# Gate projections of a two-branch mixer: spread over its units, with the results parked in DRAM

## The chip, the cores and the metric

One Trainium2 chip, one core. The metric is the device time of one execution in microseconds (us); the median of three timed runs counts. A separate execution is profiled, and all rows below come from it. Engines: PE (TensorE, matrix multiplication), DVE (VectorE), ACT (ScalarE), POOL (GpSimd), SP (the queue that issues DMAs).

## What is computed

Three blocks run one after the other on one sequence of 512 positions and 1024 channels. The change touches the third block's mixer only. It has two branches, a gated delta rule (GDN) and RWKV-7; each branch's output is multiplied by a gate that is a sigmoid of a projection of the block's input `h`, and the two are added:

```
p = h @ w_in[i]
qkv_a, z_a, b_a, a_a, p_b, gl_a, gl_b = split_cols(p, IN_SIZES)
y_a = gated_deltanet(qkv_a, z_a, b_a, a_a, conv_gdn[i], a_log[i], dt_bias[i], onorm_gdn[i])
y_b = rwkv7_time_mix(p_b, mu_rwkv[i], w0[i], w2[i], a0[i], a2[i], g2[i], k_k[i], k_a[i],
                     r_k[i], lnx_w[i], lnx_b[i])
y_a = y_a.astype(x.dtype) @ w_branch_gdn[i]
y_b = y_b.astype(x.dtype) @ w_branch_rwkv[i]
merged = jax.nn.sigmoid(gl_a) * y_a + jax.nn.sigmoid(gl_b) * y_b
x = x + gate1 * (merged @ w_out[i])
```

`gl_a` and `gl_b` have 1024 columns each, so there are 8 + 8 gate projections of 128 columns.

## The kernel before

Everything is feature-major: a tile is 128 channels by 512 positions. A projection (`proj_h`) loads one weight of 128 × 1024 (512 KB) on SP, splits it into a high half (cast on ACT, L310) and a low half (subtraction on DVE, L312), and runs 24 matmuls of 512 columns on PE into one of three PSUM banks named `pj` (L325 to L327). The buffers hold two raw weights, three high and three low halves.

The mixer works in eight units, four pairs of heads for each branch. A unit has three steps: `a` (projections, convolution or token shift, normalisation), `b` (scores, and `tri_inv`, which inverts eight 128 × 128 triangular matrices: a 16-step solve on DVE over the transposed diagonal blocks `iv_ld`, then small matmuls on PE, the first of them at L1820) and `d` (the recurrence over four chunks). The table `MIX3` writes down the order in which the steps are emitted: `ra0` is RWKV, step a, pair 0; `gd3` is GDN, step d, pair 3. `s0` to `s7` are the gate projections of the RWKV branch (weights 39 to 46), `t0` to `t7` those of the GDN branch (weights 31 to 38), `u0` to `u3` the merges of the RWKV branch's output. `PR3` gives each kind a number; emission is moved ahead by that number in the scheduler's priorities (`ahead`), and the scheduler then sets the order on each engine. On each engine instructions run in that order.

A gate is `sigmoid_of`: ACT takes Abs (L426, from PSUM), Exp (L429), Ln (L430), DVE the log-sigmoid (L434, from PSUM), ACT the last Exp (L1551). Before the change the results are written where they are used: `gr` (RWKV) in a state tile `s8z[2]`, in `lo`, `sg1`, `sg2` and one tile of the kind `f2`; `gg` (GDN) in two `f2` tiles, an `f4` tile and a state tile. All these are in use by the units for most of the mixer. The names in the trace are without the kernel's digits: `s`, `s_lo`, `s_sg` and `x_gate` are gate tiles, `x_yp` the split branch outputs, `ps_pj` a projection's bank. After the last unit the GDN branch is merged (8 merges of 12 matmuls), the sum is split into `hh` and `hl`, and `w_out` is applied.

Of the kernel before, what the change touches and what calls it, by code (L numbers as in the profile page):

```python
# [10 lines left out]
F32 = mybir.dt.float32  # L11
# [18 lines left out]
TAKE2 = 1  # L30
TAKE3 = 2
FILL2 = [4, 6, 8, 8]
PR3 = {"a": 0, "b": 400, "d": 500, "s": 300, "p": 150, "t": 300, "u": 0}
MIX3 = ("ra0 rb0 ra1 rd0 ga0 rb1 gb0 rd1 ra2 rb2 gd0 ga1 gb1 rd2 ra3 rb3 gd1 ga2 gb2 rd3 ga3 s0 s1 s2"
        " s3 gb3 s4 gd2 s5 s6 u0 t0 s7 u1 u2 u3 t1 t2 t3 t4 t5 t6 gd3 t7").split()

# [193 lines left out]
def dview(t, off, dims):  # L232

    return bass.AP(tensor=t.tensor, offset=t.offset + off, ap=[list(t.ap[0])] + [list(d) for d in dims])


class K:
# [1374 lines left out]
    def mix3(self):  # L1612
        nc, tc, I = self.nc, self.tc, self.I
        W = I["w_in_3"]
        stt = nc.vector.scalar_tensor_tensor
        with ExitStack() as st:
# [6 lines left out]
            with ExitStack() as sx:  # L1623
# [4 lines left out]
                f2 = lambda: self.p3.tile([P, S], F32, tag="f2", name="x3_gate", bufs=4)  # L1628
                s4 = lambda i: [self.s8z[i].rearrange("p (a b) c t -> p a (b c t)", a=4)[:, j, :] for j in range(4)]
# [10 lines left out]

                gr, gg, up = None, None, None
                for k in MIX3:
                    if k[0] == "s":
                        if gr is None:
                            gr = s4(2) + [self.lo, self.sg1, self.sg2, f2()]
                        m = int(k[1])
                        with self.ahead(PR3["s"]):
                            self.sigmoid_of(gr[m], self.proj_h(W[39 + m]))
                        continue
                    if k[0] == "t":  # L1650
                        if gg is None:
                            f4 = self.p3.tile([P, 2, S], F32, tag="f4", name="x3_gate2", bufs=2)
                            gg = [f2(), f2(), f4[:, 0, :], f4[:, 1, :]] + s4(self.niv % 2)
# [44 lines left out]
    def small3(self):  # L1698

        nc, I = self.nc, self.I  # L1700
        W = I["w_in_3"]
        p3, tmp = self.p3, self.tmp
        tt, stt, act, ts = nc.vector.tensor_tensor, nc.vector.scalar_tensor_tensor, nc.scalar.activation, nc.vector.tensor_scalar
# [20 lines left out]
        e = tmp("s3_e")  # L1724
# [14 lines left out]
        gr = self.gr = p3.tile([40, S], F32R, name="s3_gr")  # L1739
# [27 lines left out]
        h = slice(0, 64)  # L1767
# [10 lines left out]
        act(sg1, sg1, AF.Exp)  # L1778

        zt = lambda name, shape: p3.tile(shape, F32, name=name)  # L1780
        self.lc, self.xd = zt("iv_lc", [P, 32, 32]), zt("iv_xd", [P, 32, 32])
        self.Y = [zt("iv_Y0", [P, 8, P]), zt("iv_Y1", [P, 8, P])]
        self.x64 = zt("iv_x64", [P, 8, 64])
        self.Sb = [zt("ch_S0", [P, P]), zt("ch_S1", [P, P])]
# [6 lines left out]
    def tri_inv(self, LA):  # L1791


        nc, p3 = self.nc, self.p3
        tt, mm = nc.vector.tensor_tensor, nc.tensor.matmul
# [2 lines left out]
        self.niv += 1  # L1798
        q4 = [slice(32 * q, 32 * q + 32) for q in range(4)]
        for q in q4:  # L1800
            nc.scalar.mul(lc[q, 0:8, :], LA[q, :, 0, q], -1.0)
        iv = lambda name: p3.tile([P, 32, 32], F32, tag="iv", name=name, bufs=2)
        ld = iv("iv_ld")
        nc.vector.transpose(ld.rearrange("p t s -> p t s"), lc.rearrange("p h t -> p t h"))
        for i in range(1, 16):
            m = self.tmpd("iv_m", [P, 2, i, i])
            tt(m, dview(ld, 32 * i, [[528, 2], [0, i], [1, i]]), dview(xd, 0, [[528, 2], [1, i], [32, i]]), op=ALU.mult)  # L1807
# [376 lines left out]
```

## Time and profile before

| | |
|---|---|
| timed runs, us | 3452.67, 3456.22, 3472.29 (median 3456.22) |
| profiled execution, us | 3489.37 |
| its span, us | 3487.6 |
| mean granted TensorE clock over the span | 0.968 |
| PE, DVE, ACT busy, us | 3347.3, 2423.6, 1809.2 |
| the mixer's units, us from the start | about 2484 to 3010 |

The span is the time from the first to the last instruction. Busy time of PE is modelled at its ends, and a busy PE may still run at half of its clock, so the granted clock is read beside it (1.00 is 2.4 GHz, 0.50 is 1.2 GHz). Times in rows count from the start of the span.

### The profile page before, as it was taken

The numbers are of one execution on the slowest core, as the hardware profiler recorded it, in microseconds if no ns is written. First come the engines' busy times: TensorE is split into PE (matmuls) and PEld (weight loads), VectorE is DVE, ScalarE is ACT, GpSimd is POOL, SyncE is SP. The second block draws the span as 40 slices with busy tenths as digits, with TensorE's granted clock in tenths as the row PEclk, the third lists the DMA queues.
The fourth block names the chain that finished last, engine by engine and source line by source line (L and its number), as shares of the span: only waits on it lengthen the run. The fifth ranks groups of instructions, "written<-read, shape, count | busy, mean of one in ns | idle before, by whom it ended". The sixth has DMA issues, their size and how long they took to land.

```text
span 3487.6 us, 50543 instructions
## 1 busy us (share of the span) xinstructions
PE 3347.3 (96%) x20168; PEld 2672.4 (77%) x20168; DVE 2423.6 (69%) x3873; ACT 1809.2 (52%) x3020; POOL 123.6 (4%) x56
## 2 busy tenths in 40 slices
PE   7999999999799999999999999999899999999998
PEld 5888888888577777776787778878667667878887
DVE  6697767877789988677665465544767778565545
ACT  6566656566544555555455543334645556544434
POOL 0000000000132330000000000000000000000000
PEclk9999999999899999999999999999979989999999
DMA  6233333321121223334322245542201101323332
GB/s 224 91 96 100 97 95 96 107 85 56 44 72 61 68 72 97 121 106 130 100 73 67 85 135 184 171 151 97 96 23 50 40 31 38 109 90 95 95 96 85
DMA packets 109662, 325.08 MB, mean 93 GB/s; under 512 B 12721, under 2 KB 13361, under 8 KB 108786
## 3 DMA queue, kind: packets, MB, share of 16 engines
q1 hardware_dynamic: 109170, 321.06, 28.6%
q8 instruction: 158, 2.59, 0.3%
q0 software_dynamic: 256, 0.79, 0.1%
q14 instruction: 78, 0.64, 0.1%
HBM read 315.51 MB, written 6.29 MB: 92 GB/s over the span
## 4 chain that ended last, share of the span: by engine, by line
PE 76%; DVE 15%; ACT 4%; DMA 2%; issue 2%; SPq 0%; POOL 0%; DVEq 0%; ACTq 0%
PE ps_pj L326 19%; PE ps_pj L325 19%; PE ps_pj L327 19%; DMA ada_raw<-ada_w 2%; DVE w_lo L312 2%; DVE iv_m L1807 1%; PE ps_o L1443 1%; PE ps_mx L2098 1%; DVE ada_acc L493 1%; ACT w_hi L310 1%; PE ps_ad L496 1%; DVE iv_xd L1808 1%; PE ps_mx L326 1%; DVE cv_ul L318 1%; PE ps_mx L327 1%
## 5 line engine op out<-in xcount | busy, mean ns | idle before, releaser
L325 PE MATMUL ps_pj<-hh,w_hi 128*128 128x512 f32 x2344 | 940.0, 402 | 19.9 <-ACT hh L397 18.9
L326 PE MATMUL ps_pj<-hl,w_hi 128*128 128x512 f32 x2344 | 938.0, 400 | 0.0
L327 PE MATMUL ps_pj<-hh,w_lo 128*128 128x512 f32 x2344 | 934.8, 399 | 0.0
L310 ACT CAST w_hi<-w_raw 128x1024 fp32r<-128x1024 f32 (+1 forms) x435 | 454.6, 1045 | 761.5 <-PE ps_pj L326 661.4
L312 DVE TENSOR_TENSOR w_lo<-w_raw,w_hi 128x1024 fp32r<-128x1024 f32 (+1 forms) x387 | 469.9, 1215 | 312.9 <-ACT w_hi L310 305.9
L325 PEld LDWEIGHTS ps_pj<-hh,w_hi 128*128 128x128 f32 x2344 | 446.5, 191 | 130.1 <-ACT hh L397 24.5
L326 PEld LDWEIGHTS ps_pj<-hl,w_hi 128*128 128x128 f32 x2344 | 446.6, 191 | 101.3 <-issue 11.5
L327 PEld LDWEIGHTS ps_pj<-hh,w_lo 128*128 128x128 f32 x2344 | 446.0, 190 | 101.2 <-issue 10.9
L493 DVE SCALAR_TENSOR_TENSOR ada_acc<-ada_raw,sv_t_c,ada_acc 128x512 f32<-128x512 f32 x224 | 167.2, 746 | 55.0 <-DMA ada_raw<-ada_w 53.3
L967 DVE SCALAR_TENSOR_TENSOR xT<-ps_pj,ad,xT 128x512 f32<-128x512 f32 x128 | 95.4, 748 | 156.9 <-PE ps_pj L327 156.4
L312 POOL TENSOR_TENSOR w_lo<-w_raw,w_hi 128x1024 fp32r<-128x1024 f32 x48 | 121.1, 2523 | 1175.6 <-ACT w_hi L310 1175.6
L909 DVE SCALAR_TENSOR_TENSOR ps_mx<-cv_ut,vec,ps_mx 128x448 f32<-128x448 f32 (+3 forms) x192 | 128.1, 668 | 1.9 <-PE ps_mx L327 1.0
L909 DVE SCALAR_TENSOR_TENSOR ps_ad<-cv_ut,vec,ps_ad 128x480 f32<-128x480 f32 (+2 forms) x192 | 128.3, 668 | 1.6 <-ACT ps_ad L898 0.5
L325 PE MATMUL ps_pj<-w_hi,hh 128*128 128x256 f32 x416 | 120.3, 290 | 0.8 <-ACT hh L397 0.6
L327 PE MATMUL ps_pj<-w_hi,hl 128*128 128x256 f32 x416 | 118.7, 287 | 2.5 <-DVE hl L398 2.5
L326 PE MATMUL ps_pj<-w_lo,hh 128*128 128x256 f32 x416 | 121.0, 292 | 0.0
L326 PE MATMUL ps_pj<-m_yl,w_hi 128*128 128x512 f32 x256 | 100.4, 392 | 0.0
L325 PE MATMUL ps_pj<-m_yh,w_hi 128*128 128x512 f32 x256 | 100.3, 392 | 0.0
L327 PE MATMUL ps_pj<-m_yh,w_lo 128*128 128x512 f32 x256 | 100.3, 392 | 0.0
L327 PEld LDWEIGHTS ps_pj<-w_hi,hl 128*128 128x128 f32 x416 | 80.7, 195 | 3.9 <-DVE hl L398 3.2
L325 PEld LDWEIGHTS ps_pj<-w_hi,hh 128*128 128x128 f32 x416 | 80.8, 194 | 3.1 <-ACT hh L397 1.4
L326 PEld LDWEIGHTS ps_pj<-w_lo,hh 128*128 128x128 f32 x416 | 80.8, 194 | 1.9 <-issue 1.1
(793 smaller groups left out, 6486.9 us busy)
## 6 DMA issues: line engine op xcount, KB each, us to landing
ada_raw<-ada_w SPq DMA_DIRECT2D x288, 256.0 KB, 3.1
w_raw<-w_in SPq DMA_DIRECT2D x97, 512.0 KB, 3.7
w_raw<-hgrn_w_in SPq DMA_DIRECT2D x64, 512.0 KB, 3.7
w_raw<-w_mlp SPq DMA_DIRECT2D x64, 512.0 KB, 3.7
w_raw<-conv_w_in SPq DMA_DIRECT2D x48, 512.0 KB, 3.7
w_raw<-w_ffn_in SPq DMA_DIRECT2D x44, 512.0 KB, 3.5
w_raw<-hgrn_w_v SPq DMA_DIRECT2D x16, 512.0 KB, 3.6
w_raw<-hgrn_w_out SPq DMA_DIRECT2D x16, 512.0 KB, 3.6
```

Source lines behind the costliest of these rows:

```text
L310: nc.scalar.copy(hi, raw)
L312: (nc.gpsimd if self.on_pool else nc.vector).tensor_tensor(lo, raw, hi.bitcast(F32), op=ALU.subtract)
L318: self.nc.vector.tensor_tensor(lo, src, hi.bitcast(F32), op=ALU.subtract)
L325: mm(out, wh, xh, start=first, stop=False)
L326: mm(out, wh, xl, start=False, stop=False)
L327: mm(out, wl, xh, start=False, stop=last)
L493: nc.vector.scalar_tensor_tensor(acc, raw, cond[:, k:k + 1], acc, op0=ALU.mult, op1=ALU.add)
L496: nc.tensor.matmul(col[:, b:b + 1], acc[:, 128 * b:128 * b + 128], self.c("ones")[:, 0:1], start=True, stop=True)
L909: stt(o, x, tap(j), o, op0=ALU.mult, op1=ALU.add)
L967: self.nc.vector.scalar_tensor_tensor(self.xT[:, m, :], acc, gate[:, m:m + 1], self.xT[:, m, :], op0=ALU.mult, op1=ALU.add)
L1443: mm(out[64 * g:64 * g + 64, 128 * s:], vt[:, s, 128 * b + 64 * g:128 * b + 64 * g + 64], pts[g][:, c:c + S - 128 * s], start=b == 0 and s ...
L1807: tt(m, dview(ld, 32 * i, [[528, 2], [0, i], [1, i]]), dview(xd, 0, [[528, 2], [1, i], [32, i]]), op=ALU.mult)
```

## The change

`MIX3` gets a new order in which the gates stand between the units' steps from the beginning on, and `PR3` gives them −50, which lets them be taken later than what stands around them. As their final tiles are not free that early, 14 of the 16 gates are written to a tile `x_park` (one buffer, 2 KB a partition) and stored in DRAM (`g_spill`). At `S` the eight RWKV gates are loaded into their tiles, at `T` the first six GDN gates; `t6` and `t7` come behind `T` and go straight into theirs. The room for `x_park` comes from `iv_lc`, which shrinks from 32 × 32 to 8 × 32 a partition; the transpose into `iv_ld` reads its eight blocks four times instead of eight blocks and 24 blocks of zeros.

```diff
-PR3 = {"a": 0, "b": 400, "d": 500, "s": 300, "p": 150, "t": 300, "u": 0}
+PR3 = {"a": 0, "b": 400, "d": 500, "s": -50, "p": 150, "t": -50, "u": 0}
-        " s3 gb3 s4 gd2 s5 s6 u0 t0 s7 u1 u2 u3 t1 t2 t3 t4 t5 t6 gd3 t7").split()
+        " s7 ga3 S t1 gb3 t2 gd2 t3 u0 t4 u1 t5 u2 u3 T t6 gd3 t7").split()
...
+        self.parked = [self.dram.tile([P, S], F32, name="g_spill%d" % m) for m in range(16)]
...
-                    if k[0] == "s":
-                        if gr is None:
-                            gr = s4(2) + [self.lo, self.sg1, self.sg2, f2()]
+                    if k == "T":
+                        f4 = self.p3.tile([P, 2, S], F32, tag="f4", name="x3_gate2", bufs=2)
+                        gg = s4(self.niv % 2) + [f4[:, 0, :], f4[:, 1, :], f2(), f2()]
+                        for m in range(6):
+                            nc.sync.dma_start(gg[m], self.parked[8 + m])
+                        continue
+                    if gg is not None and k[0] == "t":
                         m = int(k[1])
                         with self.ahead(PR3["s"]):
-                            self.sigmoid_of(gr[m], self.proj_h(W[39 + m]))
+                            self.sigmoid_of(gg[m], self.proj_h(W[31 + m]))
                         continue
...
+                    if k[0] in "st":
+
                         m = int(k[1])
-                        with self.ahead(PR3["t"]):
-                            self.sigmoid_of(gg[m], self.proj_h(W[31 + m]))
+                        with self.ahead(PR3[k[0]]):
+                            e = self.p3.tile([P, S], F32, tag="park", name="x3_park", bufs=1)
+                            self.sigmoid_of(e, self.proj_h(W[(39 if k[0] == "s" else 31) + m]))
+                            nc.sync.dma_start(self.parked[m + (0 if k[0] == "s" else 8)], e)
+                        continue
+                    if k == "S":
+                        gr = s4(2) + [self.lo, self.sg1, self.sg2, f2()]
+                        for m in range(8):
+                            nc.sync.dma_start(gr[m], self.parked[m])
                         continue
...
-        self.lc, self.xd = zt("iv_lc", [P, 32, 32]), zt("iv_xd", [P, 32, 32])
+        self.lc, self.xd = zt("iv_lc", [P, 8, 32]), zt("iv_xd", [P, 32, 32])
...
-        nc.vector.transpose(ld.rearrange("p t s -> p t s"), lc.rearrange("p h t -> p t h"))
+        nc.vector.transpose(dview(ld, 0, [[32, 32], [8, 4], [1, 8]]), dview(lc, 0, [[1, 32], [0, 4], [32, 8]]))
```

Three places show how the program order moves. The first is DVE directly behind the last GDN output (`x_y<-ps_ad` of `gd3`); L434 is a gate's log-sigmoid, L312 a weight's low half, L318 a split of `y`. Before:

```order
L318 TENSOR_TENSOR x_yp<-x_y,x_yp 128x512
L312 TENSOR_TENSOR w_lo<-w_raw,w_hi 128x1024
L434 SCALAR_TENSOR_TENSOR x_gate_25686<-ps_pj,x_gate_25686 128x512
L312 TENSOR_TENSOR w_lo<-w_raw,w_hi 128x1024
L434 SCALAR_TENSOR_TENSOR s_0_21024<-ps_pj,s_0_21024 128x512
L312 TENSOR_TENSOR w_lo<-w_raw,w_hi 128x1024
L434 SCALAR_TENSOR_TENSOR s_0_21024<-ps_pj,s_0_21024 128x512
L312 TENSOR_TENSOR w_lo<-w_raw,w_hi 128x1024
L434 SCALAR_TENSOR_TENSOR s_0_21024<-ps_pj,s_0_21024 128x512
L312 TENSOR_TENSOR w_lo<-w_raw,w_hi 128x1024
L1571 TENSOR_TENSOR x_gate<-x_gate,ps_pj 128x512
L434 SCALAR_TENSOR_TENSOR s_0_21024<-ps_pj,s_0_21024 128x512
```

The same place of the change, from that output on (L2016 there):

```order
L2016 SCALAR_TENSOR_TENSOR x_y<-ps_ad,vec_20837,gd_gz 128x512
L312 TENSOR_TENSOR w_lo<-w_raw,w_hi 128x1024
L318 TENSOR_TENSOR x_yp<-x_y,x_yp 128x512
L434 SCALAR_TENSOR_TENSOR x_gate<-ps_pj,x_gate 128x512
L312 TENSOR_TENSOR w_lo<-w_raw,w_hi 128x1024
L434 SCALAR_TENSOR_TENSOR x_gate<-ps_pj,x_gate 128x512
L1572 TENSOR_TENSOR s_0_21040<-s_0_21040,ps_pj 128x512
```

Five gates stood behind the last unit's output, two stand there now. The second place is SP at the beginning of the mixer, from the last of the small loads on. Before:

```order
L274 DMA cst_b3s<-cst_b3s 128x392
L308 DMA w_raw<-w_in 128x1024 x33
L308 DMA w_raw<-w_br_r 128x1024
L308 DMA w_raw<-w_in 128x1024 x2
L308 DMA w_raw<-w_br_r 128x1024 x3
```

And of the change (L1661 is a store of a parked gate, L1666 a load at `S`; `g_spill_91` is `s0`):

```order
L274 DMA cst_b3s<-cst_b3s 128x392
L308 DMA w_raw<-w_in 128x1024 x7
L1661 DMA g_spill_91<-x_park 128x512
L308 DMA w_raw<-w_in 128x1024 x3
L1661 DMA g_spill_92<-x_park 128x512
L308 DMA w_raw<-w_in 128x1024 x5
L1661 DMA g_spill_93<-x_park 128x512
L308 DMA w_raw<-w_in 128x1024
L1661 DMA g_spill_94<-x_park 128x512
L308 DMA w_raw<-w_in 128x1024 x8
L1661 DMA g_spill_95<-x_park 128x512
L308 DMA w_raw<-w_in 128x1024 x2
```

Stores, which wait for ACT, now stand between the weight loads. The third place is ACT of the change near the end of the units, where three gates (`t1` to `t3`) follow closely; in brackets stands what an instruction waits for (DMAHW is a DMA's landing, for `x_park` that of the store before). Before, the gates there wait for no DMA.

```order
L1552 ACTIVATE x_park<-x_park 128x512 [waits DVE_49]
L310 CAST w_hi<-w_raw 128x1024 [waits DMAHW6_49]
L1811 ACTIVATE iv_lc<-s_1_21041 32x256 [waits DVE_49]
L1811 ACTIVATE iv_lc<-s_1_21041 32x256 x3
L310 CAST w_hi<-w_raw 128x1024 [waits DMAHW7_49,PE_49]
L426 ACTIVATE x_park<-ps_pj 128x512 [waits DMAHW2_49,PE_49,Activation_49]
L429 ACTIVATE x_park<-x_park 128x512 [waits Activation_49]
L430 ACTIVATE x_park<-x_park 128x512 [waits Activation_49]
L1552 ACTIVATE x_park<-x_park 128x512 [waits DVE_49]
L310 CAST w_hi<-w_raw 128x1024 [waits DMAHW3_49,PE_49]
L310 CAST w_hi<-w_raw 128x1024 [waits DMAHW4_49,PE_49]
L426 ACTIVATE x_park<-ps_pj 128x512 [waits DMAHW5_49,PE_49,Activation_49]
```

A gate's first operation on `x_park` waits for the store of the gate before it, and it stands in ACT's queue ahead of weight casts.

## Rows read from the trace of the kernel before

**Rows 1.** The page: span, busy time of engines, chain that ended last.

```profile
span 3487.6 us, 50543 instructions
...
PE 3347.3 (96%) x20168; PEld 2672.4 (77%) x20168; DVE 2423.6 (69%) x3873; ACT 1809.2 (52%) x3020; POOL 123.6 (4%) x56
...
PE 76%; DVE 15%; ACT 4%; DMA 2%; issue 2%; SPq 0%; POOL 0%; DVEq 0%; ACTq 0%
```

**Rows 2.** Windows of block 3's mixer: busy time (instructions), granted clock, DMA.

```profile
core 0: us, PE busy (x) PEld busy (x) DVE busy (x) ACT busy (x) POOL busy (x), PEclk, DMA share, GB/s
2484.00:3010.00 526.00, 493.26 (x4220) 365.99 (x4220) 393.11 (x781) 293.67 (x580) 1.62 (x3) 0.90 0.14 43
3010.00:3060.00 50.00, 48.53 (x213) 39.44 (x211) 29.34 (x38) 26.28 (x37) 0.00 (x0) 1.00 0.42 143
3060.00:3104.00 44.00, 44.00 (x195) 36.38 (x194) 21.27 (x28) 13.78 (x17) 0.00 (x0) 1.00 0.30 100
```

**Rows 3.** PE's waits, 2484 to 3010: releaser, us in total, times, longest.

```profile
PE ps_mx L1820 <- DVE iv_xc L1810: 9.4, 7, 3.7
PE ps_pa L1881 <- DVE rw_B L2064: 6.4, 2, 4.6
PE ps_ad L1978 <- DVE gd_y L1976: 3.8, 3, 1.7
```

**Rows 4.** Windows of 10 us in the units.

```profile
2550.00:2560.00 10.00, 6.14 (x215) 5.29 (x216) 9.77 (x15) 7.58 (x16) 0.00 (x0) 0.69 0.06 20
2560.00:2570.00 10.00, 10.00 (x85) 7.10 (x85) 2.77 (x5) 4.48 (x10) 0.00 (x0) 0.50 0.18 54
2570.00:2580.00 10.00, 10.00 (x42) 7.51 (x41) 2.99 (x5) 3.15 (x6) 0.00 (x0) 0.50 0.00 0
2580.00:2590.00 10.00, 10.00 (x36) 7.47 (x36) 4.03 (x8) 1.79 (x4) 0.00 (x0) 0.50 0.00 0
2590.00:2600.00 10.00, 10.00 (x34) 6.83 (x34) 5.20 (x8) 3.35 (x8) 0.00 (x0) 0.50 0.01 2
2600.00:2610.00 10.00, 10.00 (x37) 6.72 (x36) 6.29 (x11) 4.82 (x11) 0.00 (x0) 0.75 0.00 0
...
2870.00:2880.00 10.00, 10.00 (x24) 6.25 (x23) 3.42 (x10) 1.14 (x4) 0.00 (x0) 0.50 0.01 2
```

**Rows 5.** DVE's and ACT's waits, 2484 to 3010.

```profile
DVE s L2100 <- PE ps_mx L2098: 26.3, 14, 10.5
DVE s L1939 <- PE ps_mx L1937: 15.2, 9, 4.9
...
ACT w_hi L310 <- PE ps_pj L326: 42.0, 16, 8.9
```

**Rows 6.** Timeline of DVE: last GDN output, and gates behind it (first, second, last).

```profile
3010.26 0.75 DVE L2006 SCALAR_TENSOR_TENSOR x_y<-ps_ad,vec,gd_gz 128x512 f32<-128x512 f32 x1
...
3015.23 0.69 DVE L434 SCALAR_TENSOR_TENSOR x_gate<-ps_pj,x_gate 128x512 f32<-128x512 f32 x1 [0.59 <-ACT x_gate L430]
...
3020.67 0.69 DVE L434 SCALAR_TENSOR_TENSOR s<-ps_pj,s 128x512 f32<-128x512 f32 x1 [0.59 <-ACT s L430]
...
3037.47 0.68 DVE L434 SCALAR_TENSOR_TENSOR s<-ps_pj,s 128x512 f32<-128x512 f32 x1
```

**Rows 7.** Groups on PE by line, 3060 to 3100: x count, busy us, mean ns.

```profile
L325 PE MATMUL ps_pj<-hh,w_hi 128*128 128x512 f32 x58 | 22.6, 389 | 0.0
```

**Rows 8.** Tile `x_gate`, 2880 to 3062: duration min/median/max in ns.

```profile
L429 ACT ACTIVATE x_gate<-x_gate x5: 630/632/634, 2954.0 to 3013.9; 128x512 f32<-128x512 f32 x5
...
L434 DVE SCALAR_TENSOR_TENSOR x_gate<-ps_pj,x_gate x5: 674/682/692, 2960.6 to 3015.2; 128x512 f32<-128x512 f32 x5
```

**Rows 9.** The page's groups: the two halves of a weight.

```profile
L310 ACT CAST w_hi<-w_raw 128x1024 fp32r<-128x1024 f32 (+1 forms) x435 | 454.6, 1045 | 761.5 <-PE ps_pj L326 661.4
L312 DVE TENSOR_TENSOR w_lo<-w_raw,w_hi 128x1024 fp32r<-128x1024 f32 (+1 forms) x387 | 469.9, 1215 | 312.9 <-ACT w_hi L310 305.9
```

**Rows 10.** DMA issues (KB each, us to landing), and SP's longest wait, 2484 to 3010.

```profile
ada_raw<-ada_w SPq DMA_DIRECT2D x288, 256.0 KB, 3.1
...
xT<-x_spill SPq DMA_DIRECT2D x2, 2048.0 KB, 8.3
...
out_dram<-xT SPq DMA_DIRECT2D x8, 256.0 KB, 2.1
...
SPq L308 <- DVE w_lo L312: 350.9, 32, 32.7
```

**Rows 11.** Tile `iv_lc`: memset and transposes, ns.

```profile
L1804 DVE STREAM_TRANSPOSE iv_ld<-iv_lc x8: 1912/1963/2066, 2527.0 to 2939.3; 128x1024 f32<-128x1024 f32 x8
...
L1787 DVE MEMSET iv_lc<- x1: 912/912/912, 2464.8 to 2464.8; 128x1024 f32 x1
```

More of the change, by code (lines that the diff above doesn't have):

```diff
@@ L32 @@
 FILL2 = [4, 6, 8, 8]
-PR3 = {"a": 0, "b": 400, "d": 500, "s": 300, "p": 150, "t": 300, "u": 0}
-MIX3 = ("ra0 rb0 ra1 rd0 ga0 rb1 gb0 rd1 ra2 rb2 gd0 ga1 gb1 rd2 ra3 rb3 gd1 ga2 gb2 rd3 ga3 s0 s1 s2"
-        " s3 gb3 s4 gd2 s5 s6 u0 t0 s7 u1 u2 u3 t1 t2 t3 t4 t5 t6 gd3 t7").split()
+PR3 = {"a": 0, "b": 400, "d": 500, "s": -50, "p": 150, "t": -50, "u": 0}
+MIX3 = ("ra0 s0 rb0 s1 ra1 rd0 s2 ga0 rb1 s3 gb0 rd1 ra2 rb2 s4 gd0 ga1 s5 gb1 rd2 ra3 rb3 s6 gd1 ga2 t0 gb2 rd3"
+        " s7 ga3 S t1 gb3 t2 gd2 t3 u0 t4 u1 t5 u2 u3 T t6 gd3 t7").split()
 def fm_vec(v):
@@ L1642, in mix3 @@
                 for k in MIX3:
-                    if k[0] == "s":
-                        if gr is None:
-                            gr = s4(2) + [self.lo, self.sg1, self.sg2, f2()]
+                    if k == "T":
[5 more added lines that the diff above has]
+                    if gg is not None and k[0] == "t":
                         m = int(k[1])
                         with self.ahead(PR3["s"]):
-                            self.sigmoid_of(gr[m], self.proj_h(W[39 + m]))
+                            self.sigmoid_of(gg[m], self.proj_h(W[31 + m]))
                         continue
[L1650 to L1653, printed above, removed]
+                    if k[0] in "st":
                         m = int(k[1])
-                        with self.ahead(PR3["t"]):
-                            self.sigmoid_of(gg[m], self.proj_h(W[31 + m]))
+                        with self.ahead(PR3[k[0]]):
[7 more added lines that the diff above has]
+                            nc.sync.dma_start(gr[m], self.parked[m])
                         continue
@@ L1800, in tri_inv @@
         for q in q4:
-            nc.scalar.mul(lc[q, 0:8, :], LA[q, :, 0, q], -1.0)
+            nc.scalar.mul(lc[q], LA[q, :, 0, q], -1.0)
         iv = lambda name: p3.tile([P, 32, 32], F32, tag="iv", name=name, bufs=2)
         ld = iv("iv_ld")
-        nc.vector.transpose(ld.rearrange("p t s -> p t s"), lc.rearrange("p h t -> p t h"))
+        nc.vector.transpose(dview(ld, 0, [[32, 32], [8, 4], [1, 8]]), dview(lc, 0, [[1, 32], [0, 4], [32, 8]]))
         for i in range(1, 16):
@@ L1815, in tri_inv @@
         c16 = c32("iv_b")
-        tt(c16, lc[:, 0:8, :], self.c("m16").unsqueeze(1).to_broadcast([P, 8, 32]), op=ALU.mult)
+        tt(c16, lc, self.c("m16").unsqueeze(1).to_broadcast([P, 8, 32]), op=ALU.mult)
         ps = self.bank("mx", [P, 8, 32])
```

## The prediction, made before the changed kernel had run

> **What bounds the kernel now.** I read the summary of engines first: PE is busy for 96% of a span of 3487.6 us, DVE for 69%, ACT for 52% [rows 1]. A busy PE alone says little, so I went on to the chain that ended last: 76% of it is PE, 15% DVE, 4% ACT. The change touches block 3's mixer alone, so the next view is the table of windows over that stretch [rows 2]. It has three parts. From 2484 to 3010 us the eight mixer units run: PE is busy 493.26 of 526 us (32.7 us idle), at a mean granted clock of 0.90, with DVE busy 393.11 and ACT 293.67. From 3010 to 3060, and to 3104, PE is almost never idle and the clock is 1.00: there every projection taken away shortens the span one for one, as long as its data are there.
>
> Who ends PE's idle time in the units is in the table of waits [rows 3]. Three kinds hold 19.6 of the 32.7 us: the triangular inversion's first matmul waits for the transposed solve `iv_xc` (9.4 us in 7 waits), a transpose waits for RWKV's `rw_B` (6.4 us, 4.6 in one), and the delta rule waits for `gd_y` (3.8 us). All are waits for DVE; in each of them a projection could run, if one stood ahead of the waiting matmul in PE's queue.
>
> The windows of 10 us show the second loss [rows 4]. From 2560 to 2600 the granted clock is 0.50, the 1.2 GHz level, with PE busy all the time; it fell in the slice in which PE had waited for the first inversion and rose while PE worked on. The same shows at 2870. And the other way round DVE and ACT wait for PE: DVE 26.3 us on RWKV's scores and 15.2 us on the delta rule's, ACT 42.0 us in front of weight casts that need a buffer which PE still reads [rows 5]. So the units are bound by PE and DVE in turns.
>
> **What the change removes, adds and moves.**
>
> *The tail.* Behind the last delta-rule output (L2006, 3010.26) five gates still end, at 3015.23, then every 5.44 us, to 3037.47 [rows 6]. That 5.44 us is PE's time for a projection of 24 matmuls: in a dense stretch 3 × 58 matmuls of that shape stand in 40 us, 0.23 us each [rows 7]. In the changed order two gates stand behind that output. Three leave: 3 × 5.44 = **16.3 us off**. The 16 merges of RWKV's and the delta rule's outputs stay, so do t6 and t7, which cover the last split of `y` (0.69 us of DVE and as much of ACT).
>
> *The units.* The same 16.3 us of PE now come before 3010. Nothing of them costs time if they fit into the 32.7 us of idle; all of it does if they don't. Bounds of the sum: 0 and −16.3 us. To choose, I counted in PE's order, between each unit's last score matmul and the first matmul of its inversion, how many projection matmuls stand there for PE to do: before 71, 72, 85, 60, 48, 61, 76, 60 in the eight units, after 66, 89, 66, 90, 44, 85, 81, 53, and the last unit gets 32 more merge matmuls. Four units get 17 to 30 more (3.9 to 6.9 us at 0.23), so their waits of one to two us should go, and two further gates stand ahead of the scores of the unit with the 4.6 us wait. Against that three units lose 4 to 19. I take 10 of the 16.3 us as absorbed, the middle between the wait kinds' 19.6 us and none; 6.3 us make the units longer. Net **−10 us**.
>
> *A gate's other work.* One gate costs DVE 0.682 us for the log-sigmoid [rows 8] and 1.215 us for the weight's low half, ACT 4 × 0.63 us and a cast of 1.045 us [rows 9]. The number of gates is the same; three more lie within the units: 5.7 us of DVE against 133 us in which DVE is idle there. And by DVE's order eight gates stand ahead of the seventh inversion, where none stood: that is 15.2 us of DVE moved forward, out of the last units. I set both to 0; if the cover (PE-bound stretches) is gone they are +5.7 us.
>
> *DMA.* 14 stores and 14 loads of 256 KB are new. A store of that shape lands in 2.1 us, a load of that size in 3.1 [rows 10]; 7.3 MB more at a DMA share of 0.14 delays nobody. On SP each store waits for ACT's last exponential, and the weight loads wait behind it. But SP waits 350.9 us in these units for buffers already [rows 10]: in ACT's order the parked gate's last instruction stands ahead of the cast that releases the next weight load in nine of 14 cases, and 2 to 8 instructions behind it in five. Cost 0; if the cover is gone, two prefetched weights (10.9 us of PE) stand between it and PE. Parked loads are issued a unit ahead of their merge. The load of `xT` (8.3 us) now stands behind all `w_br_g` weights; the merges behind it last longer (64 + 32 matmuls, 22 us). Cost 0, at worst 8.3.
>
> *The small tiles.* `iv_lc` shrinks to a quarter: its memset of 0.912 us falls to about a quarter, −0.7 us, where DVE is the busy engine. The transpose `iv_ld` (1.963 us) [rows 11] moves as many elements with another pattern: 0 in either direction; if the broadcast pattern doubled it, +15.7 us over eight.
>
> Sum against the profiled execution: 3489.4 − 10 − 0.7 = 3478.7 us. That execution is 33.2 us above the median of the timed runs, 3456.2, and I know of no row that puts this into the mixer, so I subtract the same: 3445.5 us, say **3445**.
>
> A price of the Trainium skill stands against one row. The row: a 256 KB store lands in 2.1 us [rows 10]. The Trainium skill, page "DMA: Bandwidth & Descriptors", section "Anatomy of one DMA — SWDGE (gpsimd) path", gives about 2.0 us fixed plus bytes / 436e3, mostly the receipt of the target memory, HBM the heaviest: as an estimate by that page 2.6 us; the trace's 2.1 is used here, and the hand-over below would cost 34 us by the page's figure.
>
> **The rivals.**
>
> *The clock comes back (faster).* If gates break one of the half-clock stretches, as that of 2550 to 2610, it returns 10 × (0.31 + 4 × 0.50 + 0.25) = 25.6 us [rows 4]: 3445 − 26 = **3419**. For it: 28 more projection matmuls between the first two inversions. Against it: the scores of that stretch keep their neighbours, only five projection matmuls come between them. The Trainium skill, page "TensorE: Matmul & The Clock Gate", section "HAM oscillation — how this bites in real kernels", has the clock halve after idle gaps and tells one to keep PE fed, which speaks for this rival; the trace agrees that the clock falls at a wait and not in the dense tail.
>
> *Gates only change places (same).* PE, DVE and ACT wait for one another in turns [rows 3, 5]; what PE does earlier, DVE and ACT wait for. Nothing absorbed: **3456**.
>
> *The park buffer's hand-over (slower).* `x_park` has one buffer. ACT's first operation on the next gate (L426) waits until the store before has landed, 2.1 us after its issue, and behind it in ACT's queue stand the weight casts, the inversion's copies and all else, for which PE waits. 13 hand-overs × 2.1 = 27.3 us: 3445 + 27 = **3472**. It decides from 0.8 us each, where it eats the 10.7. Against it: ACT has other work between two gates, nine instructions or more in eight of the 13 cases, four or five in three, and in the last two a pair of weight casts of 1.045 us each, which leaves no more than a few tenths of a us to wait.
>
> **How the numbers follow.** A measurement of this kernel tells about 0.5% from nothing: 17.3 us, so below 3439 is faster, above 3473.5 slower. Forecast 0.47, clock 0.20, changing places 0.20, hand-over 0.13. Faster: the clock case and some 0.13 of the forecast's own spread (all 16.3 us absorbed gives 3439), 0.33; slower: most of the hand-over and a little of the transposes and DVE, 0.13; same 0.54. The range goes from the clock case with a few us more, 3415, to just under the hand-over, 3470; about 0.2 is left out. The forecast's own range is 3439 to 3456.
>
> **What would show it.** Right: two log-sigmoids behind the last L2006 and some 34 us from it to the end of the merges instead of about 50; PE's idle in the units down from 32.7 to about 23 us; the stretch from the first unit to that output about 6 us longer. Wrong: ACT idle in front of L426 released by a DMA (hand-over); the units 16 us longer with PE's idle as before (places); a mean clock in the units well above 0.90 (clock); `iv_ld` above 2 us.

## The result, and the profile of the changed kernel

The changed kernel takes **3446.19 us** (median of 20 runs, 3437.94 to 3465.22) against 3460.57 us for the kernel before, run beside it (20 runs, 3452.67 to 3500.13). The ratio is 0.995, with a 95% interval of 0.9932 to 0.9968. Forecast were 3445 us and, as the likeliest class, "within 0.5%"; 14.4 us is 0.42%.

The profiled execution of it has a span of 3446.3 us at a granted clock of 0.979. Its windows are cut at the start of block 3, the last GDN output (now L2016) and the last sum of squares behind `w_out` (L351); columns as in [rows 2].

```profile
2439.93:2984.19 544.26, 517.36 (x4467) 385.99 (x4466) 437.55 (x851) 331.48 (x636) 2.30 (x4) 0.97 0.21 69
2984.19:3061.31 77.12, 73.67 (x316) 60.07 (x315) 42.76 (x56) 27.98 (x38) 0.00 (x0) 0.98 0.34 118
...
2484.00:2984.00 500.00, 478.49 (x4314) 357.06 (x4315) 399.92 (x790) 307.00 (x601) 1.61 (x3) 0.98 0.20 65
```

I call the second stretch the tail, the first the units. The same cuts in the profile of before:

```profile
2438.97:3010.26 571.29, 533.10 (x4377) 395.67 (x4376) 431.51 (x843) 320.00 (x619) 2.30 (x4) 0.90 0.15 48
3010.26:3104.30 94.04, 92.57 (x405) 75.79 (x404) 50.35 (x65) 40.09 (x55) 0.00 (x0) 1.00 0.36 122
```

The tail is 16.9 us shorter, with 89 matmuls fewer (three gates are 72). The units are 27 us shorter too, though they hold more matmuls; but their clock was 0.90 before and is 0.97 now, and the profiled execution of before lay 29 us above the median of its 20 runs. These two profiles alone can't tell a better order from a better draw of the clock, and the experiments had to.

The timeline of DVE shows what is left behind the last output, two log-sigmoids where [rows 6] have five:

```profile
2984.19 0.75 DVE L2016 SCALAR_TENSOR_TENSOR x_y<-ps_ad,vec,gd_gz 128x512 f32<-128x512 f32 x1 [0.81 <-PE ps_ad L2015]
...
2987.93 0.69 DVE L434 SCALAR_TENSOR_TENSOR x_gate<-ps_pj,x_gate 128x512 f32<-128x512 f32 x1 [0.37 <-ACT x_gate L430]
...
2993.01 0.69 DVE L434 SCALAR_TENSOR_TENSOR x_gate<-ps_pj,x_gate 128x512 f32<-128x512 f32 x1 [0.60 <-ACT x_gate L430]
```

PE's waits from 2439.93 to 3061.31 (columns as in [rows 3]; L1830 and L1988 are the L1820 and L1978 there):

```profile
PE ps_mx L1830 <- DVE iv_xc L1820: 9.9, 8, 2.3
PE ps_pj L325 <- ACT hh L397: 5.0, 1, 5.0
PE ps_pj L325 <- DVE x_gate L434: 3.5, 1, 3.5
...
PE ps_ad L1988 <- DVE gd_y L1986: 1.6, 3, 0.9
...
PE ps_pa L1891 <- DVE rw_B L2074: 0.3, 1, 0.3
```

The wait for `rw_B` fell from 6.4 to 0.3 us, that for `gd_y` from 3.8 to 1.6 us; `iv_xc` takes as long as before (9.9 against 9.4 us). The 3.5 us for `x_gate` are new: in the tail a matmul waits for the bank from which DVE still reads t7's projection.

Parking, and the small tile: the DMA issues, the two longest waits of SP's queue in the units (L1661 stores a parked gate), and the tile `iv_lc`.

```profile
g_spill<-x_park SPq DMA_DIRECT2D x14, 256.0 KB, 2.3
...
s<-g_spill SPq DMA_DIRECT2D x8, 256.0 KB, 2.9
```

```profile
SPq L308 <- DVE w_lo L312: 273.9, 35, 25.0
SPq L1661 <- ACT x_park L1552: 72.0, 14, 12.0
```

```profile
L1814 DVE STREAM_TRANSPOSE iv_ld<-iv_lc x8: 1931/1964/2085, 2528.5 to 2916.1; 128x1024 f32<-128x1024 f32 x8
...
L1797 DVE MEMSET iv_lc<- x1: 272/272/272, 2465.6 to 2465.6; 128x256 f32 x1
```

No wait of ACT for a parked store is in the trace. SP waits 72 us to issue the stores, and 77 us less than in [rows 10] for `w_lo`, in a stretch of 500 us against one of 526. The transposes take 1.964 us against 1.963 in [rows 11], the memset 0.64 us less.

### The profile page after: what moved, and what is told of

Same layout as the page of the kernel before. It is cut to its first block, busy times and chain, and to the rows that moved or that the text cites. A ratio compares the mean times of both kernels' runs of the same rounds, so it can differ in the third digit from the quotient of the medians.

```text
span 3446.3 us, 50617 instructions
## 1 busy us (share of the span) xinstructions
PE 3313.8 (96%) x20168; PEld 2647.7 (77%) x20168; DVE 2422.0 (70%) x3873; ACT 1808.1 (52%) x3020; POOL 123.6 (4%) x56
## 4 chain that ended last, share of the span: by engine, by line
PE 76%; DVE 15%; ACT 4%; issue 2%; DMA 2%; SPq 0%; POOL 0%; DVEq 0%; ACTq 0%
PE ps_pj L326 19%; PE ps_pj L325 19%; PE ps_pj L327 19%; DVE w_lo L312 2%; DMA ada_raw<-ada_w 2%; PE ps_o L1444 1%; DVE iv_m L1817 1%; ACT w_hi L310 1%; PE ps_ad L497 1%; PE ps_mx L326 1%; DVE iv_xd L1818 1%; DVE cv_ul L318 1%; PE ps_mx L724 1%; DVE ada_acc L494 1%; PE ps_mx L327 1%
## 5 line engine op out<-in xcount | busy, mean ns | idle before, releaser
L312 DVE TENSOR_TENSOR w_lo<-w_raw,w_hi 128x1024 fp32r<-128x1024 f32 (+1 forms) x387 | 470.1, 1216 | 309.3 <-ACT w_hi L310 301.9
L312 POOL TENSOR_TENSOR w_lo<-w_raw,w_hi 128x1024 fp32r<-128x1024 f32 x48 | 121.1, 2522 | 1176.0 <-ACT w_hi L310 1176.0
```

The source lines that it names most:

```text
L312: (nc.gpsimd if self.on_pool else nc.vector).tensor_tensor(lo, raw, hi.bitcast(F32), op=ALU.subtract)
```

## The experiments

The theories. **1**: the gates leave the tail, where each costs its 5.44 us, and find PE idle in the units. **2**: the gates keep the clock up in the units. **3**: the small tile and its transposes are part of the gain. **4**: gates only change places.

How the runs are read: every run has a span and a mean granted clock. Within one kernel the two go together: over 244 runs of 12 kernels the span falls by 3.0 us for each 0.001 of clock, with a correlation of -0.97. So I give each kernel's span at a clock of 0.980 (each run moved along that slope, then the mean, with its standard error), beside the median as timed. The first is a comparison of orders, the second holds the clock drawn as well. That the slope found within kernels also holds between them is an assumption. The ratio is to the kernel before, run beside each on the same chip. e1 to e4 ran on one chip, e5 to e8 on a second, e9 to e12 on a third; there the kernel before has medians of 3457.1, 3466.9 and 3461.4 us, but 3453.1, 3453.0 and 3452.8 us at a clock of 0.980. So medians compare only within a chip, the spans at 0.980 across them. One of e12's twelve runs took 16,033 us, at a granted clock of 0.188, and is left out.

| kernel | runs | median, us | mean clock | span at 0.980, us | ratio, 95% interval |
|---|---|---|---|---|---|
| before, its runs with a clock on record | 105 | 3461.1 | 0.9769 | 3453.0 ± 0.2 | |
| changed (first 20 runs and e2) | 32 | 3447.0 | 0.9787 | 3442.9 ± 0.4 | 0.995 (0.9932 to 0.9968), first 20 alone |
| e3, all gates ahead | 6 | 3435.5 | 0.9825 | 3440.2 ± 1.2 | 0.9926 (0.9902 to 0.995) |
| e4, s gates only | 12 | 3452.3 | 0.9774 | 3445.8 ± 0.7 | 0.999 (0.9972 to 1.0008) |
| e5, t gates only | 12 | 3461.0 | 0.9770 | 3451.3 ± 0.5 | 0.9996 (0.9977 to 1.0015) |
| e6, small tile only | 12 | 3460.9 | 0.9757 | 3446.6 ± 1.0 | 0.9978 (0.995 to 1.0006) |
| e7, none in first units | 12 | 3444.4 | 0.9808 | 3448.0 ± 0.8 | 0.9949 (0.9929 to 0.9969) |
| e8, early priority | 6 | 3443.4 | 0.9797 | 3440.4 ± 1.5 | 0.994 (0.9918 to 0.9962) |
| e9, strided view only | 12 | 3457.3 | 0.9781 | 3453.5 ± 0.4 | 0.999 (0.9965 to 1.0015) |
| e10, short memset, big tile | 12 | 3455.6 | 0.9778 | 3447.9 ± 0.8 | 0.9974 (0.9949 to 0.9999) |
| e11, changed, other order | 12 | 3447.1 | 0.9811 | 3448.9 ± 0.6 | 0.9956 (0.9931 to 0.998) |
| e12, all ahead, other order | 11 | 3440.7 | 0.9826 | 3447.2 ± 0.5 | 0.9936 (0.9914 to 0.9958) |

**e1, the kernel before again.** No edit.

> The kernel before once more, unchanged, so that its granted clock is drawn anew. Theory 1 (the change shortens the stretch behind the last GDN output and its gates are absorbed in the units' TensorE idle): the mean clock of the runs is like that of the changed kernel (0.978 in the middle of its 20 runs), the span is about 0.5% longer at the same clock, and a profile that does not have the half-clock stretch shows units of about 500 us and a stretch behind the last GDN output of about 94 us. Theory 2 (the change buys clock): the runs of this kernel have a mean clock lower by about 0.005 than those of the changed one, half-clock stretches stand in its units again (526 us), and span times clock is the same for both kernels. Ratio to itself 1.000.

Measured: 3458.23 us, ratio 1.0014 (0.9986 to 1.0042). Its profile has no long half-clock stretch; units and tail:

```profile
2436.32:2976.25 539.93, 500.65 (x4377) 373.53 (x4376) 431.61 (x844) 320.33 (x619) 2.31 (x4) 0.97 0.15 51
2976.25:3070.29 94.04, 92.57 (x405) 75.78 (x404) 50.35 (x65) 40.09 (x55) 0.00 (x0) 1.00 0.37 123
```

The same instructions in the same order take 540 us here and 571 us in the profile of before: the 31 us are the clock's. The tail is 94.04 us both times. The spans at an equal clock differ by 10 us between the kernels, so theory 2 can't be all of it.

**e2, the changed kernel again.** No edit.

> The changed kernel once more, unchanged. Theories 1 and 4 (gates only change places) alike: units of 495 to 530 us by the clock drawn, the stretch behind the last GDN output 77 us whatever the clock of the units. Theory 1: ratio 0.995; theory 4: 1.000. Theory 2: the clock in the units stays at 0.97 or above in each look.

Measured: 3447.62 us, ratio 0.9962 (0.9942 to 0.9982).

```profile
2435.27:2977.11 541.84, 516.27 (x4467) 385.19 (x4466) 437.73 (x852) 331.63 (x636) 2.31 (x4) 0.98 0.20 69
2977.11:3054.25 77.14, 73.69 (x315) 60.02 (x314) 42.79 (x56) 27.97 (x38) 0.00 (x0) 0.98 0.35 118
```

Beside e1, with the clock of the whole span at 0.980 in both: the tail 16.9 us shorter, the units 1.9 us longer, the span 15.1 us shorter. This is one pair, and the clock of its units differs (0.97 and 0.98); over all runs the spans at an equal clock differ by 10.1 us.

**e3, all sixteen gates ahead of the last GDN output.**

```diff
-" s7 ga3 S t1 gb3 t2 gd2 t3 u0 t4 u1 t5 u2 u3 T t6 gd3 t7"
+" s7 ga3 S t1 gb3 t2 t3 gd2 t4 u0 t5 u1 t6 u2 t7 u3 T gd3"
-                            for m in range(6):
+                            for m in range(8):
-                        with self.ahead(PR3[k[0]]):
+                        with self.ahead(-50 if k[0] == "s" else 100):
```

(In the first line `t0` moves ahead of `ga2` too.)

> All sixteen gates are parked ahead of the last GDN output, where the change leaves two behind it. Theory 1: the stretch behind it loses two more gates of 5.44 us, less a wait of some 3.5 us of TensorE for the split of the last output, so about 67 to 70 us against 77; the units take 10.9 us more of TensorE work and have 21.5 us idle, so they grow by 0 to 5 us; 3440 us, ratio 0.993 to before. Theory 4: the units grow by the 10.9 us that the stretch behind loses, ratio as the changed kernel's, 0.995. Theory 2: the clock in the units is no lower than 0.97 and the ratio 0.995 or below.

Measured: 3435.47 us, ratio 0.9926 (0.9902 to 0.995), below both kernels.

```profile
2428.06:2974.35 546.29, 517.64 (x4492) 388.44 (x4491) 440.30 (x854) 337.19 (x645) 2.32 (x4) 0.98 0.21 71
2974.35:3041.83 67.48, 66.42 (x290) 54.19 (x289) 40.75 (x54) 22.26 (x29) 0.00 (x0) 1.00 0.38 127
```

The tail lost 9.7 us, the units took 4.5 us more: as theory 1 has it. But at a clock of 0.980 it is only 2.7 us below the changed kernel, about two standard errors; 11.4 us more between the mean spans go with its higher clock (0.9825 against 0.9787).

**e4, s gates only.** The changed kernel, with `t0` to `t7` straight in their tiles, `t3` to `t7` behind `gd3` in the table; the priority of `t0` to `t2` is 0, that of the others −150.

```diff
-"... gd1 ga2 t0 gb2 rd3 s7 ga3 S t1 gb3 t2 gd2 t3 u0 t4 u1 t5 u2 u3 T t6 gd3 t7"
+"... gd1 ga2 gb2 rd3 s7 ga3 S gb3 gd2 u0 T t0 u1 t1 u2 t2 u3 gd3 t3 t4 t5 t6 t7"
```

> Only the eight gates s of the first branch are spread over the units and parked; the eight gates t go straight into their tiles, and four of them stand behind the last GDN output (before: five, changed: two). Theory 1: the stretch behind the last GDN output is about 94 - 5.4 = 88.5 us, and the gain is a third of the change's: 3455 us, ratio 0.998. Theory 2 (the gates in the first units keep the clock up, and that is the gain): the whole gain is there, ratio 0.995, with a clock of 0.97 or above in the units. Theory 4: ratio 1.000.

Measured: ratio 0.999 (0.9972 to 1.0008), tail 87.6 us as expected with four gates in it. Theory 2 in the form "the first units' gates are the gain" falls: these gates are there, the clock is that of before (0.9774), and the gain isn't. At a clock of 0.980 the span is 7.2 us below the kernel before, but e6 and e10 have as much with no gate moved: this kernel has the small tile too.

**e5, t gates only.** The s gates straight in their tiles as before, `t0` to `t5` parked with the priority 300. The end of the table:

```diff
-"... s7 ga3 S t1 gb3 t2 gd2 t3 u0 t4 u1 t5 u2 u3 T t6 gd3 t7"
+"... ga3 S s0 s1 s2 t0 s3 gb3 t1 s4 t2 gd2 s5 t3 s6 t4 u0 t5 s7 u1 u2 u3 T t6 gd3 t7"
```

> The other half alone: the eight gates s go straight into their tiles as before, six of the gates t are parked in the units; three gates stand behind the last GDN output (before five, changed two). Theory 1 (what counts is the number of gates behind the last GDN output): that stretch is 94 - 2 x 5.4 = 83 us, and at the same clock the kernel is 6 to 9 us below the one before, ratio about 0.998. Theory 4 (gates only change places): the stretch is 83 us, the units take 11 us more, ratio 1.000. Theory 2 (the gates in the first units keep the clock up): no gain here, since the first units hold no gate, ratio 1.000 with clocks as the kernel before.

Measured: ratio 0.9996 (0.9977 to 1.0015), and the tail is not 83 but 95.5 us. PE's groups in that tail, and in the tail of e9 (which has the order of before; the counts are those of one of the three lines of a projection):

```profile
L325 PE MATMUL ps_pj<-hh,w_hi 128*128 128x512 f32 x80 | 31.1, 389 | 0.0
L325 PE MATMUL ps_pj<-x_yp,w_hi 128*128 128x512 f32 x54 | 21.4, 396 | 3.5 <-DVE x_gate L434 3.5
```

```profile
L325 PE MATMUL ps_pj<-hh,w_hi 128*128 128x512 f32 x99 | 38.5, 389 | 0.0
...
L325 PE MATMUL ps_pj<-x_yp,w_hi 128*128 128x512 f32 x35 | 13.9, 396 | 1.5 <-DVE s L434 1.5
```

19 matmuls a line of gates left the tail, 19 a line of merges (out of `x_yp`) took their place. The table suggests why, though no run isolates it: `t0` to `t5` now stand ahead of `u1` to `u3` there, and their priority is 300, the merges' 0. So "gates behind the last output" is not the measure: the tail gets shorter only when work leaves it and nothing comes for it. Theory 1 as I had stated it falls here, and theory 4 holds for this order. At an equal clock e5 is 1.7 us below the kernel before, but 3 to 5 us above e6 and e10, which share its short memset.

**e6, the small tile only.** The kernel before with

```diff
-self.lc, self.xd = zt("iv_lc", [P, 32, 32]), zt("iv_xd", [P, 32, 32])
+self.lc, self.xd = zt("iv_lc", [P, 8, 32]), zt("iv_xd", [P, 32, 32])
...
-nc.vector.transpose(ld.rearrange("p t s -> p t s"), lc.rearrange("p h t -> p t h"))
+nc.vector.transpose(dview(ld, 0, [[32, 32], [8, 4], [1, 8]]), dview(lc, 0, [[1, 32], [0, 4], [32, 8]]))
```

> The kernel before with the small iv_lc tile and the transpose over strided views alone. Theory 1: the memset is 0.6 us shorter, the transposes take 1.96 us as before, the stretches are the same (units 540 us at a clock of 0.97, 94 us behind the last GDN output), ratio 1.000. Theory 3 (the smaller tile or the other reading order of the transposes is a part of the gain): transposes below 1.9 us or units shorter by 3 us and more at the same clock, ratio 0.999 or below.

Measured: ratio 0.9978 (0.995 to 1.0006), and at a clock of 0.980 the span is **6.4 us** shorter, where I had counted 0.7. The transposes take 1.944 us (min to max 1.920 to 2.033), 0.15 us less over eight, so they are not it. But the order of the instructions on PE, DVE, ACT and SP's queue is no longer that of the kernel before: a memset that is 0.64 us shorter is enough for the scheduler to place the work behind it differently. e9 and e10 take the two apart.

**e7, no gate in the first units.** The changed kernel with the s gates later.

```diff
-"ra0 s0 rb0 s1 ra1 rd0 s2 ga0 rb1 s3 gb0 rd1 ra2 rb2 s4 gd0 ga1 s5 gb1 rd2 ra3 rb3 s6 ..."
+"ra0 rb0 ra1 rd0 ga0 rb1 gb0 rd1 s0 ra2 s1 rb2 s2 gd0 s3 ga1 s4 gb1 s5 rd2 ra3 rb3 s6 ..."
```

> The changed kernel with its first gates later: none of them stands in the first two units, where the change has four. Theory 1: the stretch behind the last GDN output stays at 77 us; the units hold the same gates and take 542 to 547 us at a clock of 0.97 or more, ratio 0.996 as the changed kernel's. Theory 2: without gates in the first units the half-clock stretch behind the first of them is there in more of the runs, and the mean clock over the runs falls to that of the kernel before (0.977 to 0.978, against 0.979), which gives back 3 to 5 us, ratio 0.997 to 0.998.

Measured: ratio 0.9949, tail 77.8 us. The mean clock, 0.9808, did not fall as theory 2 wanted. Against theory 1 the span at an equal clock is 5 us above the changed kernel's, and no lower than that of e6 and e10, which park no gate: at these places the gates are worth nothing beyond what the short memset gives.

**e8, the gates' priority as before.**

```diff
-PR3 = {"a": 0, "b": 400, "d": 500, "s": -50, "p": 150, "t": -50, "u": 0}
+PR3 = {"a": 0, "b": 400, "d": 500, "s": 300, "p": 150, "t": 300, "u": 0}
```

> The changed kernel with the gates' priority as it was before (300 ahead in place of 50 behind): gates start earlier, and one in place of two stands behind the last GDN output. Theory 1: the stretch behind it is 77 - 5.4 us, about 72 us or, with the 3.5 us wait gone as well, 68 us; the units grow by 3 to 6 us; ratio 0.995. Rival, that the back priority is what keeps the gates out of the units' way: the units grow by more than the 5.4 us, as the gates now stand ahead of the units' own matmuls, and the ratio is 0.998 or above.

Measured: ratio 0.994 (0.9918 to 0.9962), tail 67.5 us. The units took 551.9 us in its profile, 10 more than e2's, but at a clock that was lower over the span (0.977 against 0.980); over its six runs the span at an equal clock is not above the changed kernel's (3440.4 ± 1.5 against 3442.9 ± 0.4). The rival falls: the back priority is not needed.

**e9, the strided view only.** Of e6's edit the transpose alone; the tile and its memset as before. Every engine's order is that of the kernel before.

> The kernel before with the transpose over strided views alone: the iv_lc tile and its memset keep their size, and every engine's instructions stand in the order of the kernel before, row for row. Spans are put to a granted clock of 0.980 by the 3.0 us per 0.001 that the runs of the kernel before show (that kernel: 3453.0 us). If the gain of the small tile came from the transposes, 3447 us; if it came from the order that its shorter memset set off, 3453 us, transposes of 1.96 us and a stretch of 94.0 us behind the last GDN output.

Measured: 3453.5 us at 0.980 against 3453.0, transposes 1.972 us, tail 94.05 us. The view does nothing.

**e10, a short memset on the big tile.** e9 with only the first eight rows of `iv_lc` set to zero.

```diff
-for t in (self.lc, self.xd, self.x64, *self.Y, *self.Sb, *self.s8z):
+nc.vector.memset(self.lc[:, 0:8, :], 0.0)
+for t in (self.xd, self.x64, *self.Y, *self.Sb, *self.s8z):
```

> The kernel before with the iv_lc tile at its old size and the strided views, but only its first eight rows set to zero: the same 0.6 us less of VectorE as with the small tile, and an order that differs from that of the kernel before and from that of the small tile too. If the order is what moves the time, TensorE's waits ahead of the first unit (3.0 us for s_rw, 8.0 us for hh in the kernel before) change again, and the span at a clock of 0.980 lies anywhere in 3443 to 3458 us; if the tile's size or the room it frees is, 3453 us.

Measured: 3447.9 us at 0.980, 5.6 us below e9, with the tile at its old size. Its order did not come out as expected: on PE, DVE, ACT and SP's queue the instructions stand in the order of e6, one for one. So e6 and e10 are one order twice, with tiles of two sizes and the same time within the noise (3446.6 ± 1.0 and 3447.9 ± 0.8). Units and tail of e9:

```profile
2437.03:2975.55 538.52, 499.12 (x4377) 371.26 (x4376) 431.41 (x843) 320.24 (x619) 2.31 (x4) 0.97 0.15 51
2975.55:3069.60 94.05, 92.58 (x405) 75.80 (x404) 50.37 (x65) 40.09 (x55) 0.00 (x0) 1.00 0.37 123
```

and of e10:

```profile
2430.37:2961.74 531.37, 500.14 (x4377) 373.86 (x4376) 428.85 (x844) 320.69 (x619) 2.31 (x4) 0.97 0.15 52
2961.74:3055.79 94.05, 92.58 (x406) 75.77 (x404) 50.35 (x65) 40.09 (x55) 0.00 (x0) 1.00 0.37 123
```

PE's idle time in the units is 39.4 us in e9 and 31.2 in e10, with not a gate moved. Of PE's waits in e9, these two

```profile
PE ps_mx L1820 <- DVE iv_xc L1810: 9.4, 7, 3.6
...
PE ps_mx L1753 <- ACT s_rw L1747: 3.0, 1, 3.0
```

became, in e10, the first of these, and the second of e9 is gone; the wait for `rw_B` stays:

```profile
PE ps_mx L1821 <- DVE iv_xc L1811: 6.9, 6, 1.7
PE ps_pa L1882 <- DVE rw_B L2065: 6.3, 2, 3.7
```

That is 5.5 of the 8.2 us; the rest is the balance of smaller waits that went both ways. So it is the order that the short memset sets off, not the tile.

**e11 and e12, the changed kernel and e3 in another order.** Both with two more memsets of the small tile (0.27 us each), which bring the sum of its memsets to 0.82 us, near the 0.91 of before.

```diff
+nc.vector.memset(self.lc, 0.0)
+nc.vector.memset(self.lc, 0.0)
```

> The changed kernel with two more memsets of the small iv_lc tile, 0.27 us of VectorE each, which do nothing but draw the order anew (two gates still behind the last GDN output). If the gain comes from where the gates stand: 77 us behind the last GDN output, 3443 us at a clock of 0.980 give or take the 3 to 6 us that an order is worth, ratio 0.994 to 0.998. If the changed kernel's gain is a lucky order: 3447 to 3453 us.

> The kernel with all sixteen gates ahead of the last GDN output, with the same two idle memsets. If the place of the gates counts: 67 to 68 us behind the last GDN output, 3440 us at a clock of 0.980 give or take 3 to 6 us, below the changed kernel in the same order; if the order alone does it, no nearer to 3440 than the run with two gates behind.

Measured: e11 3448.9, e12 3447.2 us at 0.980. Units and tail of e11, then of e12:

```profile
2435.77:2980.18 544.41, 514.99 (x4464) 382.11 (x4463) 439.38 (x854) 331.18 (x636) 2.31 (x4) 0.98 0.20 67
2980.18:3058.01 77.83, 74.38 (x319) 60.61 (x318) 42.90 (x56) 28.09 (x38) 0.00 (x0) 0.98 0.36 125
```

```profile
2439.80:2987.93 548.13, 516.82 (x4484) 383.81 (x4483) 441.64 (x854) 337.35 (x645) 2.31 (x4) 0.99 0.21 69
2987.93:3057.25 69.32, 68.45 (x299) 55.85 (x298) 41.57 (x56) 22.35 (x29) 0.00 (x0) 1.00 0.38 137
```

e11 lies within what both theories had allowed, so by itself it decides nothing; e12 is 1.7 us below e11 (two standard errors) but 7 us above e3, more than the 3 to 6 us that I had given an order. Put together with the others, spans at a clock of 0.980:

| memsets of `iv_lc` | gates as before | 14 parked (changed) | 16 parked |
|---|---|---|---|
| long (0.91 or 0.82 us) | 3453.0, 3453.5 (e9) | 3448.9 (e11) | 3447.2 (e12) |
| short (0.27 us) | 3446.6 (e6), 3447.9 (e10) | 3442.9 | 3440.2 (e3) |

From left to right the gates are worth 4 to 5 us and then 2 to 3 more, in each row; from the upper row to the lower one the order is worth 5 to 7, in each column. But each cell is one order, and the rows are not one cause: e9 loses its time at `s_rw` and `iv_xc`, e11 at halves of weights (`w_lo` and `w_hi`), for which PE waits in its units

```profile
PE ps_pj L327 <- DVE w_lo L312: 3.4, 3, 2.4
PE ps_pj L325 <- ACT w_hi L310: 2.9, 2, 2.6
```

and which cost 0.6 us in e2, all of it for `w_lo`. And with 14 parked and the short memset three orders give 3440.4 (e8), 3442.9 (changed) and 3448.0 us (e7). So 4 to 5 us is what the gates brought in these two pairs of orders; an order alone is worth as much.

## Why the prediction came out right

Its time was right, in part by luck: its sum had two terms of the wrong size that made up for one another, a third part of the gain was not in it, and its base, the median of three runs (3456.2), lay 4.4 us below that of twenty (3460.57). From the kernel before to the changed one, spans at an equal clock fall by 10.1 us (predicted: 10.7). The mean clock rises from 0.9769 to 0.9787, which at 3.0 us per 0.001 is another 5.4 us. Together 15.5, and the mean spans differ by 15.4 us (3462.2 to 3446.8). The 5.4 are the least certain part: on the one chip where both kernels ran with their clocks on record these were 0.9776 and 0.9788, or 3.6 us, with a standard error of nearly 3.

- **The tail, -16.3 us.** Measured -16.9, in two profiles of each kernel, whatever the clock in the units. The last of the five log-sigmoids ([rows 6]) came 5.92 us behind the fourth and not 5.44, which changes nothing in the sum. Right, though it holds a wait that I had not seen coming: t7's bank, 3.5 us. In e3 it is gone.
- **The units, +6.3 us, with 10 of 16.3 absorbed.** This is the term that failed. PE's idle in the stretch of [rows 2] fell from 32.7 to 21.5 us, as the prediction's 23 had it, and I would have read that as proof. But e10 loses 8.2 us of idle without the gates. What the gates bring on top differs by order: idle in the units falls from 31.2 (e10) to 25.6 us (e2), or from 39.4 (e9) to 29.4 (e11), and of these 5.6 and 10.0 us the tail takes back 2.0 (it idles 3.5 where it idled 1.5). The spans have 4 to 5 us in both pairs, where the prediction had 10: the gates keep less of what leaves the tail than I took. The reason behind the 10 was half right. The gates that stand ahead of the scores did fill the wait for `rw_B` (6.3 us in e10, 0.3 in the changed kernel), and that for `gd_y` fell. The projections between scores and inversions, from which the prediction expected most, did not shorten the wait for `iv_xc`: 9.4 us before, 6.9 in e10, 9.9 in the changed kernel.
- **The small tile, -0.7 us.** The memset is 0.64 us shorter, as counted. But the term is 5 to 6 us (e6 6.4, e10 5.1), since the shorter instruction changes the order of what stands behind it. The prediction costed the instruction and not what the scheduler makes of it.
- **Transposes, DVE, DMA, SP, `xT`: 0.** Transposes 1.964 us against 1.963. Stores land in 2.3 us, loads in 2.9, the DMA share rose from 0.14 to 0.20, `xT` took 8.4 us against 8.3. All at 0 in the changed kernel, as far as these runs can tell. In the second order they are not all: PE's waits for halves of weights there (3.4 and 2.9 us in e11) have no term in the sum, and whether the stores among the weight loads cause them was not isolated.
- **The base.** I took off the 33.2 us by which the profiled execution stood above the median and wrote that no row puts them into the mixer. The subtraction was right, the sentence was wrong: e1 and e9 run the units in 540 and 539 us, not 571, and the half-clock stretch of [rows 4] is where it went. Of the 105 runs three have a mean clock as low as that profile's 0.968.
- **The clock rival (3419).** Its price was taken from a stretch that most executions don't have, and so was already out of the median. The prediction's sign for it, a clock in the units well above 0.90, came (0.97), but e1 has it without the change. What the clock did give is the 3.6 to 5.4 us above. Its other half holds: of the 79 runs of the six kernels that park gates of both branches (changed, e3, e7, e8, e11, e12) 3 have a mean clock below 0.975, of the 165 runs of the other six 42. The Trainium skill, page "TensorE: Matmul & The Clock Gate", section "HAM oscillation — how this bites in real kernels", has the clock fall after waits and asks to keep PE fed; these counts agree with it in direction. But PE's idle in the units does not order the clocks: e10 and e12 have 31 us each, and mean clocks of 0.9778 and 0.9826. Which wait it is was not isolated: e4 fills the first units and has the clock of before, e7 leaves them empty and has the higher one.
- **Gates only change places (3456).** Nearly: of the 16.9 us that leave the tail 4 to 5 are kept at an equal clock; in e7 and e5, against e6 and e10, nothing is.
- **The hand-over (3472).** Fell: no wait of ACT for a store.

What stays open: how much of the 4 to 5 us belongs to the gates in any order and how much to these orders (a few more orders of the same kernels would tell); why parking gates of both branches goes with fewer low clocks; and why the order after the short memset loses fewer waits, which is shown only as far as the two waits above. A second buffer for the parked tile was not tried.

## What to carry over

Work that moves off a dense stretch into another counts only by the idle time that it fills there, so read the gain from PE's idle over both stretches, never from the one that got shorter, and hold it against the spans. Where a scheduler sets the order, an edit of half a microsecond can be worth six: before a small gain is put down to the idea behind it, run the idea's parts alone and the idea in a second order. And where the clock wanders from run to run, compare spans at an equal clock; the medians then show what the clock added. The version with all sixteen gates ahead of the last output (e3, 3435.47 us) is below both kernels, and in the second order (e12) below the changed kernel in that order (e11), by 1.7 us at an equal clock.

## What the runs showed of the hardware

The half-clock stretch is drawn anew in each execution, and not at one place. The profile of before has it at 2560 to 2600 [rows 4], e1 and e9, with the same order, have no long one, and e6 has it three inversions later:

```profile
2700.00:2710.00 10.00, 7.84 (x96) 5.72 (x95) 9.97 (x15) 4.03 (x7) 0.00 (x0) 1.00 0.07 27
2710.00:2720.00 10.00, 9.66 (x161) 7.32 (x163) 3.28 (x11) 2.42 (x6) 0.00 (x0) 0.64 0.16 56
2720.00:2730.00 10.00, 10.00 (x93) 8.04 (x89) 3.07 (x10) 3.48 (x7) 0.00 (x0) 0.50 0.00 0
2730.00:2740.00 10.00, 10.00 (x43) 7.56 (x43) 2.82 (x5) 4.33 (x11) 0.00 (x0) 0.50 0.16 54
2740.00:2750.00 10.00, 10.00 (x24) 5.76 (x23) 2.83 (x7) 2.51 (x7) 0.00 (x0) 0.50 0.00 0
2750.00:2760.00 10.00, 10.00 (x33) 7.33 (x31) 6.12 (x17) 3.23 (x8) 0.00 (x0) 0.50 0.00 0
```

In e6 it begins behind a 10 us slice in which PE idles 2.2 us, and PE then works for 40 us at 1.2 GHz without a gap that the slices show. From one inversion's `iv_xc` to the next it takes 81.5 us with such a stretch in the profile of before (first to second), where e1, the same kernel, takes 62.7; and 81.8 us in e6 (fourth to fifth), where e10, with the same order, takes 57.3.
